# Two norm weights loaded as rows and spread by TensorE, in the input stage of a hybrid decoder block

## The chip, the cores and the metric

The kernel runs on one core of a Trainium2 chip. A core has TensorE (PE, with PEld for its weight loads), VectorE (DVE), ScalarE (ACT), GpSimd (POOL) and SyncE (SP, which here issues nearly all the loads), each with an instruction queue of its own that is worked off in order, and 16 DMA engines that they share. The metric is the device time of one execution in microseconds; the median over several executions counts. The profile is of one execution, and its span runs from the first instruction to the last.

## The reference

One decoder block on 1024 tokens of 1024 channels, all in float32: a state-space branch and a forgetting-attention branch read one normalised input, are gated and merged; then cross-attention into 256 memory tokens, a SwiGLU layer, and a last norm. What the change touches is the beginning:

```
def rms_norm(x, gain):
    y = xf * lax.rsqrt(jnp.mean(xf * xf, axis=-1, keepdims=True) + RMS_EPS)
    return (y * gain)
...
u = rms_norm(h, norm_mix[l])
proj = u @ w_in[l]
...
memory_cross_attention(..., rms_norm(mem, norm_mem_kv[l]), ...)   # k, v = split(m @ w_kv)
```

So the input stage normalises 256 memory tokens with the weight vector norm_mem_kv and 1024 tokens with norm_mix, both of 1024 channels, forms the keys and values of the memory, and the part of the input projection that the state-space branch reads.

## The kernel before

Products of full precision are made of three products of parts: each operand is split into a high part, rounded to TensorE's reduced float32 (a cast on ScalarE, L182), and a low part, the rest (a subtraction on VectorE, L183). `mm3` (L170 to L174) adds high x high, low x high and high x low.

The input stage (`stage_in`, from L344) works on ten tiles of 128 tokens by 1024 channels: memory tiles m and n, and tiles 0 to 7. A tile is loaded (F), its squares are summed on ScalarE (Q, L372), the root is taken on VectorE and GpSimd (R, L192 to L212), the tile is scaled by the root and the norm's weight on VectorE (S, L225; tiles 6 and 7 on ScalarE and GpSimd), turned on TensorE by eight products with the identity (T, L231, in two halves 0 and 1), and taken out of PSUM in high and low parts (E). Weight blocks are loaded (D) and split (W): blocks 0 to 3 for the keys (K, then k takes them out), 4 to 7 for the values (V, v), 8 to 11 for the state-space input (U, u). G loads a norm's weight vector, 0 for norm_mem_kv and 1 for norm_mix; y stores keys and values; L and P belong to the parameters of the state-space branch (L1192 to L1222, which turns them on TensorE at L1214 and L1221); X runs idle products with the identity (L250).

The order in which these steps are written is the string `ORDER_IN`. A scheduler then places the instructions on each engine's queue; a step that is written `behind` others is placed after them there. PSUM has banks of four kinds: three mm, two sc, two pv, one misc. All loads of the stage stand in SP's queue, and a load also waits for the one eight places ahead of it, and where its buffer is reused for the last reader of that buffer: of the weight buffers (raw) there are four, so block 4 waits for the split of block 0, block 5 for that of block 1.

A norm's weight is loaded by one DMA that reads the 4 KB vector for each of the 128 partitions, 512 KB into a tile:

```
S.dma_start(gain[i], (g_kv if i == 0 else g_mix).partition_broadcast(P))
```

## Time and profile before

| | |
|---|---|
| median of 3 runs | 1548.62 us (1547.12 to 1548.8) |
| the profiled execution | 1548.85 us |
| its span | 1547.1 us, 20406 instructions |
| TensorE busy | 1523.0 us, 98% |
| VectorE busy | 1010.4 us, 65% |
| ScalarE busy | 657.2 us, 42% |
| GpSimd busy | 255.1 us, 16% |
| moved by DMA | 235.10 MB, 152 GB/s in the mean |
| granted TensorE clock, mean | 0.997 |

A row of the windows gives a stretch of the span, its length, then the busy us and the number of instructions of PE, PEld, DVE, ACT and POOL, the granted clock, the busy share of the DMA engines (over 1 where transfers overlap) and GB/s. A row of waits gives who waited for whom, the us in total, the times and the longest. A row of the chain or of the timeline gives start and length in us, the engine, the line and what it does; in brackets the idle time ahead of it and what ended it. Lines in rows of before are those of the kernel before; in the changed kernel the same lines stand by one more up to the steps of the stage, and by some 30 more behind them.

### The profile page before, as it was taken

How to read it: one execution, taken by the hardware profiler on the slowest of the kernel's cores; microseconds unless marked ns; L12 is line 12 of the kernel's file. 1: busy time of each engine (PE TensorE's matmuls, PEld its weight loads, DVE VectorE, ACT ScalarE, POOL GpSimd, SP SyncE). 2: the span in 40 equal slices, each digit the busy share in tenths (PEclk: the TensorE clock that was granted, in tenths of full speed). 3: DMA queues.
4: the chain of work that ended last, by engine and by line, in shares of the span. 5: the costliest groups of instructions: out<-in, count | busy, mean ns of one | idle time of the engine just before them, and what ended most of it. 6: DMA issues, size and time to landing. Idle time of an engine off the chain costs nothing.

```text
span 1547.1 us, 20406 instructions
## 1 busy us (share of the span) xinstructions
PE 1523.0 (98%) x7325; PEld 1258.1 (81%) x7325; DVE 1010.4 (65%) x1824; ACT 657.2 (42%) x1178; POOL 255.1 (16%) x341
## 2 busy tenths in 40 slices
PE   8999999999999999999999999999999999999997
PEld 7788888898777678888888888888888888888886
DVE  6936554454778867675546797777777776665555
ACT  6424334323667643232425663333333333353342
POOL 1156442100211213200002200000000000100001
PEclk9999999999999999999999999999999999999999
DMA  9635557611224655369310256555554444896642
GB/s 310 160 103 103 130 121 140 190 35 17 47 47 90 172 149 185 109 202 314 110 69 1 109 205 204 160 160 161 162 160 158 156 144 146 296 391 208 195 151 108
DMA packets 196549, 235.10 MB, mean 152 GB/s; under 512 B 35592, under 2 KB 127656, under 8 KB 195936
## 3 DMA queue, kind: packets, MB, share of 16 engines
q1 hardware_dynamic: 188960, 215.97, 46.8%
q10 hardware_dynamic: 7488, 17.83, 3.1%
q8 instruction: 57, 0.93, 0.2%
q14 instruction: 44, 0.36, 0.1%
HBM read 162.98 MB, written 72.71 MB: 152 GB/s over the span
## 4 chain that ended last, share of the span: by engine, by line
PE 89%; DVE 5%; ACT 1%; issue 1%; DMA 1%; SPq 1%; POOL 0%; POOLq 0%; DVEq 0%; ACTq 0%
PE mm L898 15%; PE mm L172 9%; PE mm L174 9%; PE mm L173 9%; PE pv L898 8%; PE mm L1040 5%; PE sc L172 4%; PE sc L173 4%; PE sc L174 4%; PE sc L898 4%; PE sc L1040 4%; PE pv L1040 3%; PE misc L1040 2%; PE pv L172 1%; PE sc L1686 1%
## 5 line engine op out<-in xcount | busy, mean ns | idle before, releaser
L183 DVE TENSOR_TENSOR wlo<-raw,whi 128x1024 fp32r<-128x1024 f32 (+2 forms) x120 | 127.3, 1065 | 50.7 <-ACT whi L182 49.5
L182 ACT CAST whi<-raw 128x1024 fp32r<-128x1024 f32 (+2 forms) x120 | 108.5, 908 | 109.9 <-PE mm L173 41.2
L183 DVE TENSOR_TENSOR ol<-or,oh 128x1024 fp32r<-128x1024 f32 x73 | 89.9, 1234 | 73.0 <-ACT oh L182 72.3
L172 PE MATMUL mm<-uh,whi 128*128 128x512 f32 x344 | 137.2, 399 | 0.1
L173 PE MATMUL mm<-ul,whi 128*128 128x512 f32 x344 | 135.5, 394 | 0.0
L174 PE MATMUL mm<-uh,wlo 128*128 128x512 f32 x344 | 135.3, 394 | 0.0
L182 ACT CAST oh<-or 128x1024 fp32r<-128x1024 f32 x73 | 76.7, 1053 | 105.2 <-PE pv L1040 36.0
L931 POOL TENSOR_TENSOR g<-a,c 128x512 f32<-128x512 f32 x22 | 35.7, 1622 | 388.1 <-ACT a L930 388.1
L1696 POOL TENSOR_TENSOR pl<-pf,ph 128x512 fp32r<-128x512 f32 (+1 forms) x32 | 37.8, 1182 | 236.5 <-DVE ph L1695 197.3
L174 PEld LDWEIGHTS mm<-uh,wlo 128*128 128x128 f32 x344 | 65.0, 189 | 13.7 <-DVE wlo L183 0.5
L172 PEld LDWEIGHTS mm<-uh,whi 128*128 128x128 f32 x344 | 65.2, 189 | 12.0 <-DVE mc L1661 0.4
L173 PEld LDWEIGHTS mm<-ul,whi 128*128 128x128 f32 x344 | 65.2, 189 | 11.0
L202 POOL TENSOR_TENSOR r<-ms,mhalf 128x1 f32<-128x1 f32 (+1 forms) x30 | 20.4, 681 | 324.4 <-DVE ms L198 280.6
L920 DVE SCALAR_TENSOR_TENSOR c<-c,pv 128x512 f32<-128x512 f32 x22 | 15.1, 688 | 78.4 <-ACT c L919 78.4
L1693 ACT ACTIVATE pf<-sc 128x512 f32<-128x512 f32 (+1 forms) x96 | 46.4, 489 | 43.9 <-DVE sc L1689 27.8
L898 PE MATMUL pv<-S3h,we 128*128 128x512 f32 x176 | 57.8, 390 | 0.0
L1699 DVE TENSOR_TENSOR pl<-pf,ph 128x512 fp32r<-128x512 f32 (+2 forms) x64 | 35.3, 553 | 9.7 <-ACT ph L1698 9.1
L1040 PE MATMUL mm<-oh 128*128 128x512 f32 x106 | 41.3, 390 | 0.0
L1040 PE MATMUL mm<-ol,oh 128*128 128x512 f32 x106 | 41.3, 390 | 0.0
L1040 PE MATMUL mm<-oh,ol 128*128 128x512 f32 x106 | 41.3, 390 | 0.0
L172 PE MATMUL sc<-uh,whi 128*128 128x512 f32 x104 | 40.9, 393 | 0.0
L172 PE MATMUL mm<-yh,whi 128*128 128x512 f32 x104 | 40.8, 392 | 0.0
(595 smaller groups left out, 4559.3 us busy)
## 6 DMA issues: line engine op xcount, KB each, us to landing
or<-c_d SPq DMA_DIRECT2D x77, 256.0 KB
wo<-in_w_ffn_out_dram SPq DMA_DIRECT2D x22, 512.0 KB
c_d<-g SPq DMA_DIRECT2D x44, 256.0 KB
t_d<-wo SPq DMA_DIRECT2D x44, 256.0 KB
or<-t_d SPq DMA_DIRECT2D x44, 256.0 KB
rawb<-in_w_ffn_in_dram SPq DMA_DIRECT2D x20, 512.0 KB
raw<-in_w_ffn_in_dram SPq DMA_DIRECT2D x20, 512.0 KB
raw<-in_w_in_dram SPq DMA_DIRECT2D x19, 512.0 KB
```

What stands on the lines that cost most here:

```text
L172: T.matmul(ps, lh, rh, start=first, stop=False)
L173: T.matmul(ps, lh, rl, start=False, stop=False)
L174: T.matmul(ps, ll, rh, start=False, stop=last)
L182: cast = self.A.copy(hi, src)
L183: self.rest = (self.G if pool_lo else self.V).tensor_sub(lo, src, f32(hi))
L202: self.G.tensor_tensor(out=r, in0=v, in1=self.mhalf[:, 0:n], op=ALU.pow)
L898: T.matmul(ps, l_[:, k, :], r_, start=first and k == 0 and i == 0, stop=k == 3 and i == 2, skip_group_check=True)
L931: G.tensor_mul(g[:, 512:], a1, c1)
L1040: T.matmul(ps, l_[:, gi], r_[:, 512:], start=n < 3 and p == 0 and k == 0 or n == 7 and p == 0 and k == 0, stop=p == NP - 1 and k == 2, ski ...
L1693: self.exp = A.activation(pf[:, off:], ps[:, off:], AF.Exp)
L1696: G.tensor_sub(pl[:, off:], pf[:, off:], f32(ph[:, off:]))
L1699: V.tensor_sub(pl[:, off:], pf[:, off:], f32(ph[:, off:]))
```

## The change

Both weight vectors are loaded as one row of 4 KB into partition 0 of their tile (G). A new step B spreads a row over the partitions: TensorE multiplies a column of ones (a row of 128 ones as the stationary operand, plain float32) with the row, in two products of 512 columns, into two PSUM banks: mm for norm_mem_kv, sc for norm_mix. The memory tiles are scaled straight from PSUM, in two halves of 512 columns each. For norm_mix a new step C copies the two banks into the tile on ScalarE, behind the cast of the weight block last split (block 1). The squares of memory tile m are summed in two halves, one on ScalarE and one on VectorE. The 36 idle products become 10, and the turns of tile n use a bank mm in place of sc. In the order, memory tile n and block 0 are loaded ahead of norm_mix, B0 stands behind the idle products and B1 behind the turns of m, C1 ahead of token square 0, and E of m's first half ahead of the second turn of n.

```
 ORDER_IN = """
-Fm G0 Qm Fn D0 X36 Qn Rm D1 Sm F1 G1 Tm0 Tm1 Em0 Rn Sn Tn0 F0 D2 W0 Tn1 Em1 En0 En1 D3 F2 F3 W1 Q0 Q1 K0 D4 F4 F5 K1 R0
+Fm G0 Fn D0 G1 X10 B0 Qm Qn Rm D1 Sm F1 Tm0 Tm1 B1 Rn Sn Tn0 F0 D2 Em0 Tn1 W0 En0 Em1 En1 D3 F2 F3 W1 C1 Q0 Q1 K0 D4 F4 F5 K1 R0
 S0 T00 T01 k0 E00 Q2 W2 D5 F6 F7 E01 S1 T10 Q3 W3 k1 K3 K2 W4 E10 W5 D6 R1 k2 T11 k3 S2 Q4 V0 S3 T30
...
+    one = small.tile([1, P], F32, tag="one", bufs=1, name="one")
+    V.memset(one, 1.0)
     def gains(i):
         gain[i] = xtile("gain")
-        S.dma_start(gain[i], (g_kv if i == 0 else g_mix).partition_broadcast(P))
+        S.dma_start(gain[i][0:1, :], (g_kv if i == 0 else g_mix).rearrange("(o c) -> o c", o=1))
+
+    def spread_gain(i):
+        spread[i] = []
+        with B.behind(B.turning):
+            for b in range(2):
+                ps[i, "g", b] = B.bank(("mm", "sc")[i])
+                B.turning = T.matmul(ps[i, "g", b], one, gain[i][0:1, 512 * b:512 * b + 512], start=True, stop=True)
+                spread[i].append(ps[i, "g", b])
+
+    def keep_gain(i):
+        with B.behind(cast_w):
+            for b in range(2):
+                A.copy(gain[i][:, 512 * b:512 * b + 512], spread[i][b])

     def square(t):
...
+        if t == -2:
+            first = small.tile([P, 2], F32, name="ssm")
+            A.activation(junk[:, 0:512], tiles[t][:, 0:512], AF.Square, scale=1.0 / 32, accum_out=first[:, 0:1])
+            V.tensor_tensor_reduce(out=B.junk, in0=tiles[t][:, 512:], in1=tiles[t][:, 512:], scale=1.0 / D, scalar=0.0,
+                                   op0=ALU.mult, op1=ALU.add, accum_out=first[:, 1:2])
+            ss[t] = first
+            return
...
     def scale(t, pool):
         i = t // 2
         r = rs[t][:, 0:1] if t < 0 else rs[i][:, t % 2:t % 2 + 1]
-        with B.behind(turned_m if t == -1 else None):
-            scaled[t] = B.norm_scale(tiles[t], tiles[t], r, gain[0 if t < 0 else 1], pool=pool)
+        if t < 0:
+            for b in range(2):
+                h = tiles[t][:, 512 * b:512 * b + 512]
+                scaled[t] = B.norm_scale(h, h, r, spread[0][b])
+        else:
+            scaled[t] = B.norm_scale(tiles[t], tiles[t], r, gain[1], pool=pool)
```

The idle products and B are also placed one behind the other (`B.turning`). The order in which the instructions then stand differs on TensorE, VectorE, ScalarE and SP, all within the input stage. Four places:

SP's queue at the very start, before: memory tiles (xt from in_mem), the two weight vectors (gain), weight blocks (raw) and token tiles.

```order
L362 DMA xt<-in_mem_dram 128x1024
L366 DMA gain<-in_norm_mem_kv_dram 128x1024
L362 DMA xt<-in_mem_dram 128x1024
L403 DMA raw<-in_w_mem_kv_dram 128x8x128 x2
L362 DMA xt<-in_x_dram 128x1024
L366 DMA gain<-in_norm_mix_dram 128x1024
L362 DMA xt<-in_x_dram 128x1024
L403 DMA raw<-in_w_mem_kv_dram 128x8x128 x2
```

The same place of the changed kernel:

```order
L364 DMA xt<-in_mem_dram 128x1024
L372 DMA gain<-in_norm_mem_kv_dram 1x1024
L364 DMA xt<-in_mem_dram 128x1024
L433 DMA raw<-in_w_mem_kv_dram 128x8x128
L372 DMA gain<-in_norm_mix_dram 1x1024
L433 DMA raw<-in_w_mem_kv_dram 128x8x128
L364 DMA xt<-in_x_dram 128x1024 x2
L433 DMA raw<-in_w_mem_kv_dram 128x8x128 x2
```

Two loads of 128 rows became two of one row, and that of norm_mix went from behind the first token load to behind weight block 0; the order of the big loads is the same.

TensorE from the last idle product to the first key product (mh and ml are the turned memory tiles, whi and wlo a weight block), before:

```order
L250 MATMUL sc<-ident 128x256
L231 MATMUL misc<-ident,xt 128x128 x4
L231 MATMUL pv<-ident,xt 128x128 x4
L231 MATMUL sc<-ident,xt 128x128 x4
L231 MATMUL pv<-ident,xt 128x128 x4
L172 MATMUL mm<-mh_0_110,whi 128x256
```

and in the changed kernel:

```order
L252 MATMUL sc<-ident 128x256
L379 MATMUL mm<-gain,one 128x512 x2
L232 MATMUL misc<-ident,xt 128x128 x4
L232 MATMUL pv<-ident,xt 128x128 x4
L379 MATMUL sc<-gain,one 128x512 x2
L232 MATMUL mm<-ident,xt 128x128 x4
L232 MATMUL pv<-ident,xt 128x128 x4
L173 MATMUL mm<-mh_0_110,whi 128x256
```

B0 stands ahead of the turns of m, B1 between the turns of m and those of n.

ScalarE around weight blocks 4 and 5 (numbers of buffers kept, since the rows would read alike: before, raw_260 is block 4, raw_326 block 5, xt_262 and xt_264 are token tiles 4 and 5, uh are high parts of turned token tiles), before:

```order
L182 CAST uh0_0_87<-misc_300 128x2x128
L182 CAST kv_310<-mm_266 128x256
L182 CAST whi_399<-raw_260 128x1024
L372 ACTIVATE junk_109,ss2_431<-xt_262 128x1024
L182 CAST uh1_0_89<-misc_300 128x2x128
L182 CAST whi_407<-raw_326 128x1024
L182 CAST uh2_0_91<-pv_305 128x2x128
L372 ACTIVATE junk_109,ss2_431<-xt_264 128x1024
```

and in the changed kernel, where raw_250 is block 4, raw_316 block 5, and xt_252 and xt_254 are token tiles 4 and 5:

```order
L183 CAST uh0_0_87<-misc_290 128x2x128
L183 CAST kv_300<-mm_256 128x256
L183 CAST whi_389<-raw_250 128x1024
L183 CAST whi_397<-raw_316 128x1024
L183 CAST uh1_0_89<-misc_290 128x2x128
L398 ACTIVATE junk_109,ss2_421<-xt_252 128x1024
L183 CAST uh2_0_91<-pv_295 128x2x128
L398 ACTIVATE junk_109,ss2_421<-xt_254 128x1024
```

The cast of block 5 moved ahead of an evacuation of token tile 0 and of the square of token tile 4.

VectorE behind the split of block 5 (ss2_320 and ss2_431 hold the sums of squares of tiles 2 and 3, and of 4 and 5; xt_224 and xt_226 are tiles 2 and 3), before:

```order
L183 TENSOR_TENSOR wlo_408<-raw_326,whi_407 128x1024
L183 TENSOR_TENSOR ul2_0_99<-pv_305,uh2_0_91 128x2x128
L209 TENSOR_TENSOR rt2_415<-r02_414 128x2
L183 TENSOR_TENSOR ul0_0_95<-misc_337,uh0_0_87 128x2x128
L210 SCALAR_TENSOR_TENSOR rt2_415<-rt2_415,ms2_413 128x2
L183 TENSOR_TENSOR kv_311<-mm_349,kv_310 128x256
L183 TENSOR_TENSOR ul3_0_101<-pv_305,uh3_0_93 128x2x128
L211 SCALAR_TENSOR_TENSOR r02_414<-rt2_415,r02_414 128x2
L200 TENSOR_SCALAR ms2_471<-ss2_431 128x2
L225 SCALAR_TENSOR_TENSOR xt_224<-xt_224,r02_414,gain_175 128x1024
```

and in the changed kernel, with the sums of tiles 2 and 3 in ss2_310 and of 4 and 5 in ss2_421, and tile 2 in xt_212:

```order
L184 TENSOR_TENSOR wlo_398<-raw_316,whi_397 128x1024
L184 TENSOR_TENSOR ul2_0_99<-pv_295,uh2_0_91 128x2x128
L201 TENSOR_SCALAR ms2_403<-ss2_310 128x2
L201 TENSOR_SCALAR ms2_461<-ss2_421 128x2
L184 TENSOR_TENSOR ul0_0_95<-misc_327,uh0_0_87 128x2x128
L210 TENSOR_TENSOR rt2_405<-r02_404 128x2
L184 TENSOR_TENSOR kv_301<-mm_339,kv_300 128x256
L184 TENSOR_TENSOR ul3_0_101<-pv_295,uh3_0_93 128x2x128
L211 SCALAR_TENSOR_TENSOR rt2_405<-rt2_405,ms2_403 128x2
L210 TENSOR_TENSOR rt2_463<-r02_462 128x2
L212 SCALAR_TENSOR_TENSOR r02_404<-rt2_405,r02_404 128x2
```

The first step of the root of tiles 4 and 5, which needs both their sums of squares, moved ahead of three splits and of the root of tiles 2 and 3.

17 lines of the change are left out of this document (11 added, 6 removed).

## The prediction

> **What bounds the kernel now.** I read the page's busy rows first, then the table of windows over the first 40 us, then TensorE's waits, and last the chain that ended last, in order of time.
>
> ```profile
> PE 1523.0 (98%) x7325; PEld 1258.1 (81%) x7325; DVE 1010.4 (65%) x1824; ACT 657.2 (42%) x1178; POOL 255.1 (16%) x341
> 10.00:20.00 10.00, 6.76 (x42) 6.32 (x43) 8.17 (x14) 6.93 (x12) 0.70 (x1) 0.83 1.08 370
> 20.00:30.00 10.00, 9.58 (x81) 9.21 (x80) 7.66 (x12) 8.29 (x16) 0.70 (x1) 1.00 1.04 402
> 30.00:40.00 10.00, 9.01 (x49) 7.07 (x47) 10.00 (x24) 7.41 (x18) 1.71 (x1) 1.00 0.95 187
> ```
>
> TensorE (PE) is busy for 98% of the span; what it idles lies for the most part in the first 62 us, in the stage that is changed. Behind that the two programs have the same instructions in the same order, so a shift of TensorE at 62 us should reach the end unchanged. In that stage the DMA engines are full from 10 to 30 us (shares 1.08 and 1.04), and VectorE (DVE) from 30 to 40 us (10.00 of 10). TensorE's waits behind the first products, and the chain:
>
> ```profile
> PE sc L231 <- DVE xt L225: 2.8, 1, 2.8
> PE misc L231 <- DVE xt L225: 1.0, 1, 1.0
> PE misc L1214 <- PE mm L173: 0.8, 1, 0.8
> ...
> 16.82 10.66 DMA raw<-in_w_mem_kv_dram
> 27.50 1.06 ACT whi L182
> 28.59 1.23 DVE wlo L183
> ...
> 33.38 1.20 DVE xt L225
> 34.72 0.63 PE misc L231 x4
> 52.52 0.77 issue
> 53.28 0.23 PE misc L1214
> ```
>
> The chain does not run through the start. It runs through the queue of loads: weight block 5 (step W5, the second block of values) lands at 27.5 us, ScalarE (ACT) casts it, VectorE works through splits and scalings without a pause, and TensorE, which had its own work done at 33.7, turns token tile 3 at 34.72. From there it is busy to 52.5 us. So the question is how much earlier that turn comes.
>
> **The loads: -2.8 us at W5.** Two loads of 512 KB (both norm weights spread over 128 partitions by the DMA) become two of 4 KB; both stood ahead of block 5. What the loads move per us:
>
> ```profile
> 4.00:8.00 4.00, 4.00 (x23) 2.94 (x22) 1.55 (x5) 1.17 (x3) 1.27 (x4) 1.00 1.00 323
> 24.00:27.50 3.50, 3.15 (x28) 2.97 (x27) 2.34 (x6) 1.79 (x4) 0.44 (x1) 1.00 1.04 416
> ```
>
> 1.05 MB at 416 GB/s is 2.5 us, at 323 GB/s 3.2 us; I take 2.8 (some 370 GB/s, as from 10 to 20 us). It holds only if the queue never runs dry. Block 5 is issued when VectorE has split block 1, which I put at about 16.1 us; four loads then still stand ahead of it, over 5 us of transfer. So block 5 lands at 24.7.
>
> **The start: about -0.9 us.** These rows carry it:
>
> ```profile
> 4.50 1.06 ACT L372 ACTIVATE junk<-xt 128x1024 bf16<-128x1024 f32 x1 [2.41 <-DMA xt<-in_mem_dram]
> 7.08 1.28 DVE L225 SCALAR_TENSOR_TENSOR xt<-xt,r,gain 128x1024 f32<-128x1024 f32 x1
> 7.98 1.06 ACT L372 ACTIVATE junk<-xt 128x1024 bf16<-128x1024 f32 x1 [2.33 <-DMA xt<-in_mem_dram]
> 9.14 0.58 ACT L182 CAST mh<-misc 128x512 fp32r<-128x512 f32 x1
> 12.39 0.66 PE L231 MATMUL sc<-ident,xt 128*128 128x128 f32 x4 [2.84 <-DVE xt L225]
> L1661 DVE CUSTOM_DVE_ANT_0 junk<-mm,tri 128x512 bf16<-128x512 f32 x16 | 10.9, 683 | 1.6 <-PE mm L1659 1.3
> ```
>
> The first memory tile m still lands at 4.4. Its sum of squares is now two halves side by side, about 0.58 on ScalarE (as the cast of 512) and 0.68 on VectorE (as the 512-wide reduction with an accumulator), so its root is ready at 6.65 instead of 7.08. The second tile n lands near 6.2 instead of 7.95, since 0.52 MB less is ahead of it at 323 GB/s. What may eat this are the four added products of a row of ones with the weight row, plain fp32 and 512 wide. No such product stands in the trace; the nearest rows are these:
>
> ```profile
> 147.23 0.39 PE L1471 MATMUL pv<-St,Gm 128*128 128x128 f32 x2
> 147.45 0.39 PE L1470 MATMUL pv<-xg,Tt 128*128 128x128 f32 x2
> ...
> 30.41 0.39 PE L174 MATMUL sc<-whi,ml 128*128 128x512 f32 x1
> 30.64 0.40 PE L172 MATMUL sc<-whi,mh 128*128 128x512 f32 x1
> ```
>
> A plain fp32 product is two records and 0.224 us per 128 columns, so at most 0.90 us for 512; two records at the 0.23 us of the 512-wide row give at least 0.46. I take 0.90, since L1470 and L1471 are the nearest plain fp32 rows. A start falls in a slow stretch of TensorE; the idle matmuls alone, in two windows, with the count as what tells the rate:
>
> ```profile
> 1.86:4.20 2.34, 2.34 (x12) 1.00 0.94 266
> 7.40:8.40 1.00, 1.00 (x11) 1.00 1.14 334
> ```
>
> That is 12 in 2.34 us at first and 11 in 1.00 at the end, half the rate, though the column of the granted clock says 1.00 for both. So I double the price in B0, to 1.8 us. Beside this row, the Trainium skill (FP8 and Floating Point Precision, section TensorE Precision Notes) has true fp32 as four passes through the array; by that it would be 4 x 0.23 = 0.92, and the sum stays as it is.
>
> B0 (two products) then runs from 4.6 to about 8.0. The first bank is ready in time; the second holds up the second half of m, scaled by 8.75 (before: 8.36). VectorE's next work follows: n's root, then n's halves, done at about 11.95 (12.25 before). TensorE turns n's first half at about 11.4, against 12.39. If the products cost the lower bound, it is about 10.3. B1, behind m's turn, fits before n is scaled.
>
> **ScalarE: +1.05, then 1.3 lost to the order.** C1 copies the spread row of norm_mix from PSUM, two copies of 512 at a spacing of about 0.5, ahead of token square 0; half a square (0.48) is gone. Before, this stretch of ScalarE had slack:
>
> ```profile
> 16.64 1.05 ACT L182 CAST whi<-raw 128x1024 fp32r<-128x1024 f32 x1 [0.49 <-DMA raw<-in_w_mem_kv_dram]
> 19.76 1.06 ACT L372 ACTIVATE junk<-xt 128x1024 bf16<-128x1024 f32 x1 [0.33 <-DMA xt<-in_x_dram]
> 20.82 1.03 ACT L182 CAST whi<-raw 128x1024 fp32r<-128x1024 f32 x1
> 25.04 1.06 ACT L372 ACTIVATE junk<-xt 128x1024 bf16<-128x1024 f32 x1 [0.66 <-DMA xt<-in_x_dram]
> 27.50 1.05 ACT L182 CAST whi<-raw 128x1024 fp32r<-128x1024 f32 x1 [1.05 <-DMA raw<-in_w_mem_kv_dram]
> 28.72 1.06 ACT L372 ACTIVATE junk<-xt 128x1024 bf16<-128x1024 f32 x1
> ```
>
> Followed by hand through the new order, ScalarE casts W3 at 19.45 (before 20.82), the copies being paid out of the 0.49 and 0.33 of waiting for loads, and reaches W5 at 23.3, so it still waits for the load until 24.7. But the cast of W5 now stands ahead of a token evacuation and square 4, which used to run while block 5 was under way. Behind the cast come 0.27 + 1.05 + 0.27 (spacings of the same rows) and then square 5, whose sum is read 3.7 us after the landing; VectorE has the root's first step of that sum ahead of tile 2's root and of three splits. From the landing to token tile 3 scaled I count 8.5 us; it was 34.72 - 27.50 = 7.2. So 1.3 of the 2.8 us is lost, and the turn comes at 33.2: **-1.5 us**. TensorE's own work, carried along, is done at about 32.9, so it still waits, and 1.8 is the most that this place gives.
>
> Behind it, VectorE and ScalarE have the same work as before, all earlier by 1.5. The wait of 0.8 at L1214 (52.5 to 53.3) ends with VectorE's last split out of the bank that it writes:
>
> ```profile
> 52.76 0.42 DVE L183 TENSOR_TENSOR ul<-misc,uh 128x256 fp32r<-128x256 f32 x1 [0.44 <-ACT uh L182]
> ```
>
> So it moves along with that engine: 0. The 26 idle matmuls dropped ran while the first loads were under way: 0, unless the clock (below) goes with them. So 1548.85 for the profiled execution becomes 1547.35; the median of the runs is 0.23 below that execution, which gives 1547.1, and I say **1547.2**.
>
> **Rivals.**
>
> *The loads pass through whole (chance 0.20).* These times go from the median, 1548.62. If W5's place costs nothing, because square 5's sum is not what VectorE waits for, the gain is 2.8: 1545.8; if the 0.8 at L1214 closes too, 3.6: 1545.0. For it: the chain above. Against it: VectorE's 10.00 of 10 and the new order.
>
> *ScalarE becomes the bound (0.12).* If block 5 lands only 0.7 us earlier (its issue follows the split of block 1, which I have only 0.3 to 0.7 earlier), the 1.3 of W5's place outweighs it, by 0.6, and the 1.05 of copies finds no slack left: +1.6, and 1548.62 + 1.6 = 1550.2. It decides where the landing moves by less than 1.3. Against it: DMA shares over 1 say that bytes bound the landings and not issues.
>
> *The clock (0.06).* The granted clock as the trace has it:
>
> ```profile
> 15.00:16.00 1.00, 1.00 (x6) 1.00 (x7) 1.00 (x2) 1.00 (x3) 0.00 (x0) 0.50 1.18 290
> 17.00:18.00 1.00, 1.00 (x8) 1.00 (x7) 0.29 (x1) 1.00 (x2) 0.00 (x0) 0.66 1.16 349
> ```
>
> Half clock costs the 256-wide products 0.21 us each instead of 0.12, 6 in a us against the 11 above; some 18 products paid it in 3.4 us. If with 10 idle matmuls all 48 of the first two keys pay it, that is 30 x 0.095 = 2.9 us more on TensorE, less 0.9 of start and 1.0 of the wait at 34.72: +1.0, 1549.6. It is the case that ends slower, and decides from where TensorE and not VectorE is last at tile 3, some 0.3 us beyond my forecast. The Trainium skill speaks against the change here (TensorE: Matmul & The Clock Gate, section What's actually happening): full clock comes after about 3.4 us of activity, in a window that runs by itself. The half clock that the rows above show before 17.7 is short enough to agree with that length. What speaks against the rival: the four wide products keep TensorE busy in place of the idle matmuls.
>
> **How the numbers follow.** My forecast has 0.62, with 1546.3 to 1548.3 for landings that move by 2.0 to 3.2 us. Up to 0.2%, 3.1 us, a measurement of this kernel can't well be told from no change. The whole-pass rival gives half its chance beyond that, and the forecast's far end 0.05: faster 0.15. The two slower rivals lie within 0.2% but for their far ends: slower 0.04; same 0.81. The range is 1545.3 to 1549.7: it holds the whole-pass case but for its last 0.8 (0.07 left out) and the clock's case; the ScalarE case lies beyond it (0.10 left out).
>
> **What would show it.** Right: the cast of W5 waits for its load and starts near 24.7; square 5 follows 2.5 us later; TensorE turns token tile 3 near 33.2 after waiting for its scaling; two records of B0 take 1.8 us each pair or less; everything past 62 us is earlier by one constant. Wrong: no idle time of ScalarE ahead of W5 (ScalarE bounds), a half clock past 18 us, a turn of tile 3 at or before 32, or a new wait of TensorE between 35 and 62 us.

## The result and the profile after

The changed kernel takes 1551.98 us in the median of 15 runs (1548.49 to 1555.63), the kernel before 1548.56 in 15 runs beside it. The ratio is 1.0021, with an interval of 1.0015 to 1.0028: slower by 0.2%, some 3.4 us. The profiled execution took 1553.78 us (span 1552.1), 4.9 more than that of before; it lies 1.8 above its own median, so the pieces below add up to more than 3.4.

The busy row of the page and the table of windows, changed kernel:

```profile
PE 1528.8 (99%) x7307; PEld 1257.5 (81%) x7307; DVE 1016.4 (65%) x1829; ACT 658.2 (42%) x1180; POOL 256.9 (17%) x341
10.00:20.00 10.00, 9.86 (x31) 6.46 (x30) 6.64 (x11) 6.09 (x11) 0.05 (x1) 1.00 1.09 363
20.00:30.00 10.00, 9.77 (x80) 9.35 (x79) 8.82 (x14) 9.56 (x18) 0.70 (x1) 1.00 0.90 327
```

TensorE is busy for 5.8 us more with 18 matmuls fewer. From 10 to 20 us it does 31 where it did 42 (the column of the clock reads 1.00 there, but the trace's first clock record comes at 20.46, and the 256-wide products ahead of it follow each other in 0.21 us, behind it in 0.12: half rate until then). ScalarE is busy for 9.56 us of the next ten where it was for 8.29. The DMA engines, full from 20 to 30 us before (1.04, 402 GB/s), are at 0.90 and 327 (0.57 and 209 from 26 to 28): the queue of loads runs dry there. TensorE's waits:

```profile
PE pv L1502 <- ACT Tt L1437: 1.7, 1, 1.7
...
PE mm L1691 <- DVE mc L1696: 1.2, 1, 1.2
...
PE misc L1246 <- PE mm L174: 0.7, 1, 0.7
...
PE misc L232 <- DVE xt L226: 0.2, 1, 0.2
```

The waits of 2.8 for memory tile n and of 1.0 for token tile 3 are gone. In their place stand two that the kernel before does not have, and both lie far behind the changed stage: 1.7 at L1502 (149.6 us) and 1.2 at L1691 (421.6 us). TensorE's timeline at the start shows where the first gain went:

```profile
4.82 3.75 PE L379 MATMUL mm<-gain,one 1*128 1x512 f32 x4 [0.64 <-DMA gain<-in_norm_mem_kv_dram]
8.50 1.11 PE L232 MATMUL misc<-ident,xt 128*128 128x128 f32 x4
10.45 3.78 PE L379 MATMUL sc<-gain,one 1*128 1x512 f32 x4
14.16 1.12 PE L232 MATMUL mm<-ident,xt 128*128 128x128 f32 x4
15.95 0.58 PE L173 MATMUL mm<-mh,whi 128*128 128x256 f32 x1
```

Both pairs of row products take 3.75 us or more. The second stands ahead of the turn of n, so that turn starts at 14.16 (before: 12.39), though n is scaled at 12.66. ScalarE, which takes the turned tile out of PSUM, waits for it; before, and then in the changed kernel, with the cast of weight blocks 4 and 5:

```profile
13.08 0.58 ACT L182 CAST mh<-sc 128x512 fp32r<-128x512 f32 x1 [1.92 <-PE sc L231]
```

```profile
15.31 0.59 ACT L183 CAST mh<-mm 128x512 fp32r<-128x512 f32 x1 [3.65 <-PE mm L232]
...
25.97 2.01 ACT L183 CAST whi<-raw 128x1024 fp32r<-128x1024 f32 x2
```

From 15.31 on ScalarE has pauses of 0.27 and 0.44 us only, until blocks 4 and 5 are cast one behind the other, with no waiting for a load. Block 5 lay ready by then: the last of the sixteen semaphore updates of its load comes at 24.73 in the trace, and its cast starts at 26.92. Before, they came at 27.48 and 27.50. So the load landed 2.75 us earlier, and its cast began only 0.6 earlier. On TensorE, token tile 3 is turned at 35.91 (before: 34.72), with no waiting either:

```profile
35.91 0.63 PE L232 MATMUL misc<-ident,xt 128*128 128x128 f32 x4
```

Following the same TensorE instruction in both traces gives a ladder of its lateness: +1.6 us at 53, +0.8 at 115, +2.6 at 147, +2.7 at 335, +4.2 at 517, +5.1 at 546, +4.9 at the end. So there are three pieces: some 0.8 from the input stage, some 1.8 between 115 and 147 us, 1.2 at 420 us, and a rest near 546. A ladder is of one execution: TensorE's granted clock falls near 360 us in some (0.83 from 355 to 365 us in that of before, 0.84 in that of the change) and not in others (1.00), which alone is worth some 1.3 us there: a kernel below that has no such fall goes from 0.1 ahead at 335 us to 1.5 ahead at 417. So the pieces are read from 53 to 335 us and from the waits.

### The profile page after: what moved, and what is told of

The parts are those of the page before. It is cut to its first block, busy times and chain, and to the rows that moved or that the text cites. A ratio compares the mean times of both kernels' runs of the same rounds, so it can differ in the third digit from the quotient of the medians.

```text
span 1552.1 us, 20382 instructions
## 1 busy us (share of the span) xinstructions
PE 1528.8 (99%) x7307; PEld 1257.5 (81%) x7307; DVE 1016.4 (65%) x1829; ACT 658.2 (42%) x1180; POOL 256.9 (17%) x341
## 4 chain that ended last, share of the span: by engine, by line
PE 86%; DVE 6%; DMA 3%; ACT 2%; issue 2%; POOL 1%; SPq 0%; POOLq 0%; DVEq 0%; ACTq 0%
PE mm L930 15%; PE mm L173 8%; PE mm L175 8%; PE mm L174 8%; PE pv L930 8%; PE mm L1072 5%; PE sc L930 4%; PE sc L1072 4%; PE sc L173 3%; PE sc L174 3%; PE sc L175 3%; PE pv L1072 3%; PE misc L1072 2%; DMA rb<-rd_d 1%; PE pv L173 1%
## 5 line engine op out<-in xcount | busy, mean ns | idle before, releaser
L1191 POOL TENSOR_TENSOR sg<-sg,ga 128x512 f32<-128x512 f32 x16 | 29.6, 1874 | 73.0 <-DVE sg L1184 73.0
```

The costliest lines, as they stand in the source:

```text
L1191: self.B.G.tensor_mul(self.out[j][:, cs], self.out[j][:, cs], ga)
```

## The experiments

Two theories stood at first. By the one, the input stage makes the loss: the row products bring no clock, so the keys run at half rate up to 20.5 us. By the other, the stage is nearly neutral and the shift lands badly behind it. The first kernels tell these apart. In all of the kernels below the whole computation is done; idle products and extra loads write to places that nobody reads.

**The loads spread by the DMA again, without row products** (the halves and the 10 idle products stay):

```diff
-Fm G0 Fn D0 G1 X10 B0 Qm ... Tm0 Tm1 B1 Rn ... W1 C1 Q0
+Fm G0 Fn D0 G1 X10 Qm ... Tm0 Tm1 Rn ... W1 Q0
-        S.dma_start(gain[i][0:1, :], (g_kv if i == 0 else g_mix).rearrange("(o c) -> o c", o=1))
+        S.dma_start(gain[i], (g_kv if i == 0 else g_mix).partition_broadcast(P))
-                scaled[t] = B.norm_scale(h, h, r, spread[0][b])
+                scaled[t] = B.norm_scale(h, h, r, gain[0][:, 512 * b:512 * b + 512])
```

> The changed kernel, but both norm weights come again as 512 KB loads spread over 128 partitions; the four products with ones (steps B0, B1) and the two copies (C1) are gone. The halves, the new order and the 10 idle matmuls stay. Theory A (the four one-row products cost the time: they hold TensorE at half clock and push the first key product from 13.72 to 15.95 us): first key product back at 13.0 to 14.2 us, token tile 3 turned at 34.7 to 36, time 1548.0 to 1550.0, ratio to before 0.9997 to 1.0009. Theory B (the loss is made behind 60 us by whatever shifts the start, so any kernel with this order loses it): ratio stays at 1.0015 or more though the first key product is early. Theory C (the 26 idle matmuls dropped are the cause): half clock past 18 us here too, first key product near 14 us but 48 key products at half rate, ratio about 1.001 to 1.002.

Measured: 1548.22 beside 1548.57, ratio 1.0000 (0.9991 to 1.0009). On the ladder it is 1.7 us ahead of before at 115 us and 0.1 ahead at 546: without the row products the loss is gone, but a gain of the stage does not reach the end either.

**The kernel before with 10 idle products:**

```diff
-Fm G0 Qm Fn D0 X36 Qn Rm
+Fm G0 Qm Fn D0 X10 Qn Rm
```

> The kernel before with 10 idle matmuls instead of 36, nothing else. Theory C (idle matmuls are the cause): turn of m at half rate (1.1 us for four instead of 0.6), key products at half rate for 3 to 5 us longer, turn of token tile 3 at 35.5 or later, ratio 1.0007 to 1.002. Theory A (only the one-row products matter): the half clock lasts past 18 us perhaps, but TensorE waits for VectorE at tile 3 anyway, so the turn stays at 34.7 to 35.2 and the ratio at 0.9995 to 1.0006. Theory B: like A at 62 us, and a ratio that goes by what happens behind it.

Measured: 1549.12, ratio 1.0004 (0.9995 to 1.0013). On the ladder: 1.6 ahead at 115 us, 0.7 behind at 546. The number of idle products changes more than their own time: the scheduler places the turns of the tokens otherwise. What the stage wins is again lost far behind it.

**The kernel before, its idle products one row high** (36 as before, in the same order on each engine):

```diff
-        one = self.ident.bitcast(BF16)
+        one = self.ident.bitcast(BF16)[0:1, :]
```

> The kernel before with its 36 idle matmuls taken over one partition (1x128 by 1x256) instead of 128; nothing else. They last as long and keep TensorE as busy. If the height of the product is what the clock goes by (theory A's reason for the half clock of B0 and B1): 4 to 5 idle matmuls per 0.5 us to the end of the stretch, which then ends near 9.8 us instead of 8.5 and delays the turn of m, which takes 1.1 us for four turns; half clock on the key products past 18 us. If height is nothing to the clock: as before, 7 per 0.5 us from 7.5 us on, stretch over at 8.5, turns at 0.60 for four, ratio 1.0000 within 0.0005.

Measured: 1548.16, ratio 1.0000 (0.9991 to 1.0009). TensorE's timeline of this kernel:

```profile
1.87 7.86 PE L250 MATMUL sc<-ident 1*128 1x256 bf16 x36 [1.87 <-POOL ident masks.py:199]
9.65 1.11 PE L231 MATMUL misc<-ident,xt 128*128 128x128 f32 x4
15.16 0.58 PE L172 MATMUL mm<-mh,whi 128*128 128x256 f32 x1
```

Products of one row keep TensorE busy for 7.9 us and it stays at half rate (36 in that time, 0.22 us each): the turn of m behind them takes 1.11 us, as behind the row products of the changed kernel. (The Trainium skill, page TensorE: Matmul & The Clock Gate, section What's actually happening, says that the hardware doesn't count instructions and that about 3.4 us of activity bring the full clock. Here 7.9 us of it, one row high, did not; the measurement decides.) The first key product comes 1.4 us later than before, and the time is the same. A late start and a half clock up to 19.5 us cost nothing in the kernel before, where ScalarE still waits 0.48 us for block 5 and casts it at 27.30.

**The changed kernel with 24 idle products ahead of B0:**

```diff
-Fm G0 Fn D0 G1 X10 B0 Qm
+Fm G0 Fn D0 G1 X24 B0 Qm
```

> The changed kernel with 24 idle matmuls instead of 10; nothing else. At half rate 24 end near 7.4 us, so the products of B0 start there instead of at 4.8. Theory A in the form that the clock was never raised because full activity ended at 4.2 us: the four records of B0 take 1.9 us (0.93 a product) instead of 3.75, those of B1 1.9, m's turn comes near 9.5 us, the first key product near 14.0 instead of 15.95, at full clock or nearly; ratio 0.999 to 1.001. Theory A in the form that one-row products pull the clock down by themselves: B0 begins quick, B1 is back at 3.75 us, first key product at 15 to 16.5, ratio 1.001 to 1.003. Theory B: the ratio stays near 1.002 either way.

Measured: 1548.90, ratio 1.0002 (0.9993 to 1.0011). B0 now takes 1.98 us, at full clock, but behind it the clock falls: it is 0.5 from 9.73 us on, while m is still being turned. So B1 takes 3.78 us again, and the first key product starts at 15.99, as in the changed kernel. Yet the loss is nearly gone: the ladder shows 0.0 at 115 and 147 us, and only the wait of 1.2 at L1691 is still there. The clock in the first 20 us is not what costs 3.4 us.

**The changed kernel and the kernel before again, in another batch:**

> The changed kernel once more, on the chip of the first four experiments, for a second profile and a second comparison. So far the start does not explain the time: the kernel before with one-row idle matmuls started its key products 1.4 us late at half clock and took 1548.2, and the changed kernel with 24 idle matmuls started them as late as the changed kernel (15.99 us) and took 1548.9. Theory B1 (what lies behind 60 us was chance of that execution and that chip): median 1548.5 to 1550, and no wait of TensorE for Tt near 148 us. Theory B2 (the order that the scheduler chose with 10 idle matmuls, met by a start 2.2 us late, costs the 3 us each time): median 1551 to 1553, first L1419 turn at 116.1 again (0.8 behind before), and part of the loss made again between 115 and 150 us and between 400 and 550 us.

> The kernel before, once more, for a second profile: which of its times behind 60 us are the same each time. If the pieces behind 60 us are chance, then the store of the last u block, the drop of the granted clock near 355 us and the waits of TensorE between 500 and 550 us differ from the first profile by 1 us or more in all; if not, all marks are within 0.3 us of the first profile's.

Measured: the changed kernel 1552.01 beside 1548.21, ratio 1.0028 (1.0017 to 1.0039), with 2.3 at L1502 and 1.2 at L1691; one execution of the kernel before took 1548.54, and up to 370 us its TensorE marks stand within 0.3 us of those of the first profile. So the two new waits belong to the kernel and not to one execution. The first can cost more than its length: in this second profile the granted clock is 0.5 for 3.4 us from 150.8, right behind the wait, and the lateness is 3.3 at 147 and 5.1 at 335.

**The row products over all 128 rows** (zeros but for row 0 in both operands):

```diff
-    one = small.tile([1, P], F32, tag="one", bufs=1, name="one")
-    V.memset(one, 1.0)
+    one = small.tile([P, P], F32, tag="one", bufs=1, name="one")
+    V.memset(one, 0.0)
+    V.memset(one[0:1, :], 1.0)
...
+        V.memset(gain[i], 0.0)
-                B.turning = T.matmul(ps[i, "g", b], one, gain[i][0:1, 512 * b:512 * b + 512], start=True, stop=True)
+                B.turning = T.matmul(ps[i, "g", b], one, gain[i][:, 512 * b:512 * b + 512], start=True, stop=True)
```

> The changed kernel, but the products that spread the weight rows are of full height: the row of ones is the first of 128 rows of which the others are zero, and so is the weight row (VectorE fills both with zeros in its idle time ahead of 4 us). Count, form and order of the instructions on TensorE, ScalarE, GpSimd and SP are the same as in the changed kernel; VectorE has three fills more at the start. If the height of the product is what the clock goes by: B0 slow at first, clock up near 7.5 us as before the change, B1 in 1.9 us instead of 3.78, first key product at 13.8 to 14.4 us instead of 15.95, half clock over before 18 us. The time then tells what the late start costs in this order: theory A (the start costs it): 1548.5 to 1549.5, ratio 0.9995 to 1.0008. Theory B (it is lost behind 60 us whatever the start): 1551 to 1552.5, ratio above 1.0014. If height is nothing to the clock: start as in the changed kernel.

Measured: 1552.06, ratio 1.0021 (1.0012 to 1.0030). The timelines of TensorE and ScalarE in this kernel:

```profile
10.36 1.98 PE L381 MATMUL sc<-gain,one 128*128 128x512 f32 x4 [0.33 <-DMA gain<-in_norm_mix_dram]
13.67 0.39 PE L173 MATMUL mm<-mh,whi 128*128 128x256 f32 x1
35.68 0.63 PE L232 MATMUL misc<-ident,xt 128*128 128x128 f32 x4 [0.28 <-DVE xt L226]
```

```profile
26.96 1.04 ACT L183 CAST whi<-raw 128x1024 fp32r<-128x1024 f32 x1 [2.30 <-DMA raw<-in_w_mem_kv_dram]
```

With 128 rows the clock rises, B1 takes 1.98, and the first key product starts at 13.67, as in the kernel before; the time is that of the changed kernel. So an early start by itself does not bring the 3.5 us back. It is not a clean test of the input stage, though, since the fills hold up the first loads: SP waits 1.1 us for a fill ahead of the first weight row and issues weight block 1 at 4.49 (changed kernel: 2.98), and from 4 to 8 us the loads move 227 GB/s (there: 292). So block 5 lands late here, at 26.89, its cast waits for it, and token tile 3 is turned at 35.68, 0.96 later than before, behind VectorE. No kernel has both the early start and the early loads.

**The kernel before with only the halves** (square of m on two engines, memory tiles scaled in two halves from the tile that the DMA spread):

```diff
+        if t == -2:
+            first = small.tile([P, 2], F32, name="ssm")
+            A.activation(junk[:, 0:512], tiles[t][:, 0:512], AF.Square, scale=1.0 / 32, accum_out=first[:, 0:1])
...
+        if t < 0:
+            for b in range(2):
+                h = tiles[t][:, 512 * b:512 * b + 512]
+                scaled[t] = B.norm_scale(h, h, r, gain[0][:, 512 * b:512 * b + 512])
```

> The kernel before with the memory tiles squared (the first one) and scaled in halves, and nothing else: both weights by 512 KB loads, 36 idle matmuls. Theory A and the rivals of the prediction alike have this part as a small gain at the start: m's turn at 8.0 to 8.6 us (idle matmuls run to 8.5), n's first half turned some 0.6 us earlier, 11.6 to 12.0 us, first key product 12.9 to 13.3 instead of 13.72, and block 5 at 27.5 as before, so that the turn of token tile 3 stays at 34.5 to 34.9: ratio 0.9995 to 1.0005. Theory B (order chosen by the scheduler): the ratio may be off by up to 0.002 either way without a difference at the start.

Measured: 1549.63, ratio 1.0010 (1.0001 to 1.0019). Token tile 3 is turned at 36.13 (before: 34.72), the ladder shows +1.4 at 53 and at 115 us, and it keeps that to 546 (+1.3). Here a loss in the input stage, with the other order that the scheduler gives, passes through to the end.

### The piece at 147 us: where the instruction fetch falls

The state-space input is stored (u_d) and read back in another layout (xg). SP issues the first xg load when the last u_d store has landed. In most kernels that is 2.7 us behind the issue of the store, in the changed one 4.6. The table of half us, changed kernel:

```profile
97.50:98.00 0.50, 0.50 (x4) 1.00 0.76 311
98.00:98.50 0.50, 0.50 (x4) 1.00 0.06 8
...
99.50:100.00 0.50, 0.50 (x4) 1.00 0.04 16
```

The kernel before:

```profile
97.50:98.00 0.50, 0.50 (x4) 1.00 0.00 0
```

Before, nothing moves any more at 97.5. Now 0.06 of the 16 engines, that is one of them, goes on alone for two us. What went ahead of it is in the list of DMA queues for the window from 94 to 101 us of the changed kernel, and not in that of 93 to 99 of the kernel before:

```profile
q8 instruction: 1, 0.02, 1.5%
```

This is a piece of TensorE's instructions. The trace has 57 such packets of 16 KB for 14614 records of matmuls and weight loads, one for some 256, and in all 17 profiles the fourth of them starts when 898 to 913 of these records have begun, be that at 89 us or at 98. It takes one DMA engine away from the store: from 96.60 to 98.30, while it runs, the store has at most 15 packets under way at a time (before: 16), and behind it the store's last eight packets follow one by one, up to 99.91.

In the kernel before the piece is fetched at 92 us, between the two u_d stores; the changed kernel has 18 matmul and 18 weight-load records less ahead of it, so its stream reaches the next piece later, at 96 us, within the store. From there SP's queue, ScalarE and VectorE tell the rest. SP before, and then in the changed kernel:

```profile
97.73 5.25 SPq L1412 DMA_DIRECT2D xg<-u_d  x8
124.15 5.05 SPq L1400 DMA_DIRECT2D Ts<-Ts  x3
133.20 0.98 SPq L157 DMA_DIRECT2D raw<-in_w_in_dram  x2
```

```profile
100.43 3.55 SPq L1444 DMA_DIRECT2D xg<-u_d  x7
129.17 4.67 SPq L1432 DMA_DIRECT2D Ts<-Ts  x3
137.84 0.99 SPq L158 DMA_DIRECT2D raw<-in_w_in_dram  x2
```

A shift of 2.7 at the first xg load has become 5.0 at Ts and 4.6 at the gate's weights (raw). VectorE shows what made it grow, first before, then in the changed kernel:

```profile
117.76 0.42 DVE L1373 TENSOR_TENSOR d<-ES,trg_cs 128x256 f32<-128x256 f32 x1
...
123.81 0.28 DVE L1397 TENSOR_TENSOR Ts<-misc,dbc 128x128 f32<-128x128 f32 x1
```

```profile
121.75 1.10 DVE L1407 TENSOR_TENSOR EC<-d,d 128x256 f32<-128x256 f32 x1
122.88 1.26 DVE L1405 TENSOR_TENSOR d<-ES,trg_cs 128x256 f32<-128x256 f32 x1
...
128.83 0.28 DVE L1429 TENSOR_TENSOR Ts<-misc,dbc 128x128 f32<-128x128 f32 x1
```

Of the six 256-wide steps, four took 0.42 us before; now five take 1.1 to 1.3. GpSimd waits for TensorE in this place and so is late by only 0.8, VectorE's steps by 2.7, and now they meet: from 118.8 to 126.6 us the two take turns, one instruction each. ScalarE then copies Tt, which TensorE needs, behind a cast that waits for raw. Before, and then in the changed kernel:

```profile
141.33 1.05 ACT L182 CAST whi<-raw 128x1024 fp32r<-128x1024 f32 x1 [1.37 <-DMA raw<-in_w_in_dram]
...
142.77 1.04 ACT L1405 COPY Tt<-Ts 128x1024 f32<-128x1024 f32 x1
```

```profile
147.06 1.05 ACT L183 CAST whi<-raw 128x1024 fp32r<-128x1024 f32 x1 [5.24 <-DMA raw<-in_w_in_dram]
...
148.50 1.03 ACT L1437 COPY Tt<-Ts 128x1024 f32<-128x1024 f32 x1
```

The copy is 5.7 us late. Before, it ended at 143.8 and TensorE came at 147.0, a slack of 3.2; TensorE itself is late by 0.8; 5.7 - 3.2 - 0.8 is the wait of 1.7.

Three kernels move the fetch, each in another way.

**The changed kernel with more and smaller row products** (each in four of 128 columns, and two more idle products: the stream of TensorE is longer, the work nearly the same):

```diff
-Fm G0 Fn D0 G1 X10 B0 Qm
+Fm G0 Fn D0 G1 X12 B0 Qm
-                B.turning = T.matmul(ps[i, "g", b], one, gain[i][0:1, 512 * b:512 * b + 512], start=True, stop=True)
+                for c in range(0, 512, 128):
+                    e = min(c + 128, 512)
+                    B.turning = T.matmul(ps[i, "g", b][:, c:e], one, gain[i][0:1, 512 * b + c:512 * b + e], start=True, stop=True)
```

> The changed kernel with each of its four row products cut into four of 128 columns (same columns in all, so the same time on TensorE), and 12 idle matmuls instead of 10, which fit into the gap of 0.64 us ahead of B0 and keep the scheduler's order: otherwise all engines have the changed kernel's instructions in its order. TensorE's stream is 52 instructions longer, as long as before the change. Theory F (the place of the 16 KB instruction fetches is what costs): the fetch near 96 us comes near 92 us again, the u store lands 2.4 us after its issue, no wait for Tt near 148 us, the wait for the exponentials near 545 us falls from 0.6 to 1.7 us to about 0.3, with the start as late as in the changed kernel (first key product near 16 us); what stays is 0.8 from the input stage and 1.2 near 420 us: 1549.0 to 1550.2. Theory A or B2 (start and order): 1551.3 to 1552.7. Theory R: no change, as the loads are the same.

Measured: 1549.33, ratio 1.0007 (0.9998 to 1.0016). The fetch is at 89 us (the stream is 52 records longer than the changed kernel's and 16 longer than that of before), and the copy of Tt comes 0.9 us earlier than before:

```profile
141.87 1.04 ACT L1439 COPY Tt<-Ts 128x1024 f32<-128x1024 f32 x1
```

The wait at L1502 is gone; that at L1691 (1.2) is not. The ladder: -0.4 at 115 and at 147, +0.5 at 546. Since the start gained 1.2 too against the changed kernel (B0 ran partly at full clock), not all of the 2.7 us between the two is the fetch.

**The kernel before with a shorter stream and nothing else** (17 idle products of 512 columns in place of 36 of 256):

```diff
-Fm G0 Qm Fn D0 X36 Qn Rm
+Fm G0 Qm Fn D0 X17 Qn Rm
-            self.T.matmul(ps[:, :2 * P], one[:, :P], one, start=True, stop=True)
+            self.T.matmul(ps.rearrange("p (a b) -> p a b", a=2), one[:, :P], one.unsqueeze(1).to_broadcast([P, 2, 2 * P]),
+                          start=True, stop=True)
```

> The kernel before with its 36 idle matmuls of 256 columns taken as 17 of 512 (5% fewer columns, over at some 8.2 us instead of 8.5, ahead of the first scaling's end at 8.36); all else the same, in the same order. TensorE's stream is 38 instructions shorter. Theory F: the fetch of 92 us comes near 95.9, into the last u store (95.4 to 97.3): landing 3.5 us or more after the issue instead of 2.35, the fetch of 530 us comes near 535 and the wait for the exponentials near 541 us grows from 0.24 to 0.6 to 1.6: 1549.3 to 1551.5, ratio 1.0005 to 1.002, with the start and the input stage as before. All other theories: 1548.5, ratio 1.0000 within 0.0006.

Measured: 1549.24, ratio 1.0010 (1.0001 to 1.0019). With no row load and no row product in it, the fetch falls at 96 us, the xg load comes 4.6 us behind the store, and the new wait is there:

```profile
147.44 0.49 PE L1471 MATMUL pv<-xg,Tt 128*128 128x128 f32 x2 [1.43 <-ACT Tt L1406]
```

Its input stage had gained 1.2 us at 115; at 147 it is 0.4 late. This is the plainest of the runs: 19 idle products fewer, and a gain of 1.2 becomes a loss, 90 us after the last of them.

**Sixteen rows instead of one in the weight load** was meant for the other late wait (below), on the theory that a load in a single piece delays one DMA engine's queue:

```diff
-        S.dma_start(gain[i][0:1, :], (g_kv if i == 0 else g_mix).rearrange("(o c) -> o c", o=1))
+        S.dma_start(gain[i][0:16, :], (g_kv if i == 0 else g_mix).partition_broadcast(16))
```

> The changed kernel with each weight row loaded into 16 partitions instead of 1 (16 times the same 4 KB; only the first is used). All engines have the same instructions in the same order. A one-row load is a single piece, and all other loads near it are cut into 16 or a multiple. Theory R (the odd piece shifts which of the 16 DMA engines gets which part of every later transfer; that is why the spread 1/sum lands late near 419 us in every kernel with row loads, and why one part of the last u store trails): no wait of 1.2 us for the row maximum near 420 us, the u store lands within 2.5 us of its issue, and the time is 1548.5 to 1550. Theory F (TensorE has 52 instructions fewer, so its instruction fetches of 16 KB come some 4 us later and one of them meets the last u store): unchanged, 1551.3 to 1552.7, with the store again 3.5 to 4.3 us under way.

Measured: 1553.01, ratio 1.0033 (1.0020 to 1.0045). A miss: the wait of 1.2 at L1691 stays. The load in 16 pieces lands later, which makes the start 0.8 to 1.1 us later than in the changed kernel and moves the store, but the fetch is within it again: 2.0 at L1502. (The changed kernel's stream is 36 records shorter than that of before, by the page, and not 52.)

**Both edits:**

> The last two edits of the changed kernel together: rows loaded into 16 partitions, and row products cut into four with 12 idle matmuls. Theory R and F each for its part: neither the late u store nor the wait near 420 us nor the long one near 545 us; what is left is the input stage, 0.5 to 0.8 us behind before at 115 us: 1548.6 to 1549.5, ratio 1.0000 to 1.0007. If R is wrong and F right: as with the cut products alone, 1.2 us more. If both are wrong: 1551.3 to 1552.7.

Measured: 1551.12, ratio 1.0018 (1.0010 to 1.0027). The fetch is out of the way (91 us) and no wait stands at L1502; the late start of the 16 rows costs 1.9 on the ladder at 115 and 147, and L1691's 1.2 comes on top.

Four kernels keep the changed kernel's order on every engine up to 115 us and move its start. Against the changed kernel:

| kernel | first key product | lateness at 115 |
|---|---|---|
| split | -1.14 | -1.2 |
| split, one load (below) | +0.07 | +0.1 |
| 16-row load | +0.89 | +0.9 |
| 16-row load, split | +1.15 | +1.1 |

In this order the stage hands a shift of its start on whole. The loads have landed by the time ScalarE comes to them, and no wait for a load is left to take the shift up, as there was in the kernel before with one-row idle products.

### The piece at 420 us: a hiccup of SP's queue

In the attention, SP stores the reciprocals of a head's denominators (rd_d) and loads them back spread over 64 partitions (rb); VectorE multiplies with them. SP before, and then in the changed kernel:

```profile
410.25 0.35 SPq L1731 DMA_DIRECT2D rd_d<-rc  x1
411.74 0.51 SPq L1733 DMA_DIRECT2D rb<-rd_d  x1
412.64 0.40 SPq L1606 DMA_DIRECT2D raw<-in_w_in_dram  x1
```

```profile
413.06 0.36 SPq L1763 DMA_DIRECT2D rd_d<-rc  x1
414.90 0.50 SPq L1765 DMA_DIRECT2D rb<-rd_d  x1
415.46 0.57 SPq L1638 DMA_DIRECT2D raw<-in_w_in_dram  x1
```

From store to load it is 1.49 before and 1.84 after; from the load to the next issue 0.90 and 0.56. A pause of 0.35 us has moved from behind the rb load to ahead of it. VectorE and GpSimd, before:

```profile
415.57 1.21 DVE L1739 TENSOR_TENSOR num<-num,rb 64x1024 f32<-64x1024 f32 x1
415.73 2.20 POOL L1696 TENSOR_TENSOR pl<-pf,ph 128x512 fp32r<-128x512 f32 x1 [2.80 <-DVE ph L1695]
```

And in the changed kernel, with TensorE:

```profile
418.53 1.29 POOL L1728 TENSOR_TENSOR pl<-pf,ph 128x512 fp32r<-128x512 f32 x1 [2.80 <-DVE ph L1727]
418.99 1.91 DVE L1771 TENSOR_TENSOR num<-num,rb 64x1024 f32<-64x1024 f32 x1 [0.54 <-DMA rb<-rd_d]
421.56 0.44 PE L1691 MATMUL mm<-hb 68*128 68x384 f32 x1 [1.24 <-DVE mc L1696]
```

Whichever of the two starts first has its plain time (1.21 or 1.29), the second stands still until the first is done: 2.20 for GpSimd before, 1.91 for VectorE now. (The Trainium skill, SBUF — State Buffer, section Terms, says that the pair of memory ports which VectorE and GpSimd share is held for a whole instruction and that the loser blocks; these rows agree.) GpSimd's delay cost nothing. VectorE's makes the reduction behind it (mc) late, and TensorE waits 1.24. So 0.35 us on an idle queue became 1.24 on TensorE by who came first.

The wait stands in seven of the eight profiles of kernels that load the weights as rows and spread them with products (the eighth follows), and in none of the others. Their SP queue has one wait more than before: the tile that a later weight block reuses was last read by TensorE. Counted from the start, the pause lies between the 207th and the 208th instruction of SP's queue in the kernel before as in the changed one; with one instruction more ahead of it, another instruction of this place is the one held up. Two kernels try that with a load of 8 bytes more on SP.

**One load more in the split kernel:**

```diff
+        if n == 1:
+            S.dma_start(small.tile([1, 2], F32, tag="extra", bufs=1, name="extra"), g_mix[0:2].rearrange("(o c) -> o c", o=1))
```

> The changed kernel with cut row products and 12 idle matmuls (as in the run that took 1549.33), and one load of 8 bytes more on SP near 60 us, into a tile that nobody reads. All other instructions and their order are the same. Theory S (SP's stream has a hiccup of 0.34 us at a fixed place, between the wait for the stored 1/sum and the load that spreads it, because the changed kernel has one wait more on SP than the kernel before; the load comes 0.34 us late, VectorE's scaling starts after GpSimd's subtraction instead of ahead of it, takes 2.3 us instead of 1.2, and TensorE waits 1.24 us near 418 us): with one instruction more the hiccup falls into the time in which SP waits for the store anyway, the load is issued 1.49 us or less after the store instead of 1.85, the wait of 1.24 is gone, time 1547.8 to 1548.6. Rival (the row products themselves, or the banks they take, cause that wait): it stays, 1549.0 to 1549.8.

Measured: 1548.67, ratio 1.0005 (0.9996 to 1.0013). SP's queue:

```profile
411.32 0.35 SPq L1767 DMA_DIRECT2D rd_d<-rc  x1
412.74 0.50 SPq L1769 DMA_DIRECT2D rb<-rd_d  x1
```

It is 1.42 from store to load, and the wait at L1691 is gone with row loads and products all present. The time is 0.7 below that of the split kernel, taken in another batch, less than the two tell apart, and the profiled execution has a wait of 1.2 near 547 us that the split kernel has not. The trace shows the mechanism; its worth in time was not resolved.

**One load more in the kernel before:**

> The kernel before with one load of 8 bytes more on SP near 60 us, into a tile that nobody reads; nothing else. Theory S: the hiccup of SP falls between the wait for the stored 1/sum and the load that spreads it (1.84 us from store to load instead of 1.49), and the wait of TensorE of 1.24 us for the row maximum near 417 us appears, with everything ahead of 400 us as before: 1549.4 to 1549.9, ratio 1.0005 to 1.0009. Rival: no such wait, 1548.5, ratio 1.0000.

Measured: 1548.47, ratio 1.0000 (0.9992 to 1.0009). A miss: the expected wait did not come. From store to load it is 1.43, not 1.84. The extra load also turned the round of DMA semaphores by one, so that the wait for the store no longer is an instruction of its own ahead of the load. That the pause sits at a count of instructions, and that this place decides the wait, is supported by the seven profiles and by the kernel with the extra load; the forecast made from it failed in this one.

The pause is not the only one of its kind. Behind records 79, 207, 335 and so on of SP's queue, one in 128, each of the 17 profiles has a gap of 0.34 us or more (0.05 is usual from one record to the next), and a packet of 8 KB of the kind "instruction" starts 0.05 to 4.1 us behind each of them. Since 16 KB are some 256 of TensorE's records, 8 KB would be 128. So the pause is probably the change from one piece of SP's own instructions to the next; no run tests it.

### A version meant to keep the gain

**The first experiment (weights spread by the DMA, halves, 10 idle products) with 24 idle products one column wide**, which only lengthen TensorE's stream:

```diff
+            for _ in range(24):
+                self.turning = self.T.matmul(ps[:, :1], one[:, :P], one[:, :1], start=True, stop=True)
```

> A version that may beat both: halves and the changed kernel's order, but both weights by 512 KB loads (the first experiment, 1548.22), with 24 idle matmuls of a single column behind the 10, so that TensorE's stream is 48 instructions longer; order kept but for three turns of 128 columns that move past one product each. Theory F (the place of the 16 KB fetches): the first experiment was 1.7 us ahead of before at 115 us and lost 1.5 of it near 541 us, where a fetch at 536.5 us fell on the transfers of the row maxima; here that fetch comes near 532, the loss is gone, and the time is 1546.5 to 1547.3, ratio 0.9988 to 0.9993. Without theory F: 1548.2.

Measured: 1547.20 beside 1548.62, ratio 0.9993 (0.9984 to 1.0002). The fetches move to 91 and 530 us, and the 1.6 us gained at 115 are still there at 546 (1.5). It is the lowest median of all, but the interval does not exclude no gain.

All kernels side by side. Lateness is on TensorE against the profile of before; "fetch" is the microsecond in which TensorE's piece of instructions comes near the store; "store to xg" runs from the issue of the last u_d store to that of the first xg load; the waits are TensorE's (at L1502, at L1691 for mc, and the longest for pf).

| kernel | median, ratio | at 115 | fetch | store, to xg | L1502 | L1691 | pf | at 546 |
|---|---|---|---|---|---|---|---|---|
| before | 1548.56 | 0 | 92 | 95.1, 2.7 | none | none | 0.5 | 0 |
| changed | 1551.98, 1.0021 | +0.8 | 96 | 95.8, 4.6 | 1.7 | 1.2 | 0.6 | +5.1 |
| changed, again | 1552.01, 1.0028 | +0.8 | 96 | 95.9, 4.3 | 2.3 | 1.2 | 1.7 | +6.9 |
| 128 rows | 1552.06, 1.0021 | +0.5 | 96 | 95.6, 3.9 | none | 1.2 | 1.6 | +5.0 |
| 16-row load | 1553.01, 1.0033 | +1.6 | 98 | 96.7, 4.6 | 2.0 | 1.2 | 1.4 | +6.8 |
| 16-row load, split | 1551.12, 1.0018 | +1.9 | 91 | 96.9, 2.7 | none | 1.2 | 0.5 | +3.4 |
| split | 1549.33, 1.0007 | -0.4 | 89 | 94.7, 2.7 | none | 1.2 | 0.5 | +0.5 |
| split, one load | 1548.67, 1.0005 | +0.9 | 91 | 96.0, 2.7 | none | none | 1.2 | +2.2 |
| 24 idle | 1548.90, 1.0002 | 0.0 | 92 | 95.1, 2.7 | none | 1.2 | 0.5 | +1.0 |
| before, 17 wide idle | 1549.24, 1.0010 | -1.2 | 96 | 93.9, 4.6 | 1.4 | none | 0.5 | +0.7 |
| before, halves | 1549.63, 1.0010 | +1.4 | 93 | 96.4, 2.7 | none | none | 0.5 | +1.3 |
| before, one-row idle | 1548.16, 1.0000 | -0.2 | 91 | 94.9, 2.7 | none | none | 0.5 | -2.0 |
| before, 10 idle | 1549.12, 1.0004 | -1.6 | 96 | 93.5, 2.7 | none | none | 1.2 | +0.7 |
| DMA spread | 1548.22, 1.0000 | -1.7 | 96 | 93.4, 2.7 | none | none | 1.3 | -0.1 |
| DMA spread, padded | 1547.20, 0.9993 | -1.6 | 91 | 93.5, 2.7 | none | none | 0.5 | -1.5 |
| before, one load | 1548.47, 1.0000 | -0.1 | 92 | 95.0, 2.6 | none | none | 0.5 | +0.2 |

The column "store, to xg" has two values: 3.9 to 4.6 in the five profiles whose fetch comes 0.5 to 2.5 us behind the issue of the store, and 2.6 or 2.7 in the eleven whose fetch comes earlier, or (twice, 93.4 and 93.5) at 96 us when the store has landed. With 128 rows the wait at L1502 is missing although the store was late: its copy of Tt ended at 147.40, just as TensorE came.

Near 546 us the wait for pf is 1.2 or longer in six profiles. In five of them a later fetch falls between 536 and 542 us; but the kernel with 17 wide idle products has a fetch at 536 and no such wait, the first profile of the changed kernel has one at 540 and a wait of 0.6, and the split kernel with one load has the wait with its fetch at 530. No run tests this place by itself. Its cause is open.

## Why the prediction was wrong

Forecast 1547.2, measured 1551.98. The step that failed is in the first part: "Behind that the two programs have the same instructions in the same order, so a shift of TensorE at 62 us should reach the end unchanged." The order is the same, and TensorE's lateness still changed from 0.8 at 115 us to 4.9 at the end. What differs is the length of the streams: TensorE's is shorter by 18 pairs of records, so that a fetch falls into a store; SP's is longer by a wait, so that a pause falls ahead of a load. Against the forecast of -1.5, the input stage is off by 2.3 (+0.8 at 115), what lies behind it by 4.1 in the profiled execution.

The terms of the sum, in their order:

- **The loads: -2.8 us at W5.** The landing was right: 24.73 for 24.7, 2.75 earlier than before, though the load was issued at 18.98 and not at 16.1, behind VectorE's late split of block 1. What was wrong is that ScalarE would be waiting for it.
- **The start: about -0.9 us.** B0 was right: 3.75 for 3.6, with the turn of m at 8.50. B1 is the term of the stage that failed. It was priced at 1.8, full clock (it is 1.98 where the clock is full), and called free behind the turn of m. It took 3.78, since products of one row do not bring the clock, and the turn of n came at 14.16 and not at 11.4. ScalarE, waiting for that turn, casts block 1 at 16.65 (before: 14.04) and does not catch up. A start 1.4 us late cost nothing in the kernel before, but in the changed kernel's order a shift of the start passes on whole. What B1 alone is worth was not measured.
- **ScalarE: +1.05, then 1.3 lost to the order.** ScalarE casts block 3 at 22.90 and not at 19.45, and never waits for block 5: it comes to it at 26.92. That is the sign set down for the ScalarE rival ("no idle time of ScalarE ahead of W5"). From there to the turn of token tile 3 it is 9.0 us, 8.5 foreseen, so that the turn comes at 35.91 and not at 33.2.
- **The wait of 0.8 at L1214 moves along: 0.** About right: 0.7, 1.6 us later.
- **26 idle matmuls dropped: 0, unless the clock goes.** Wrong in a way that neither branch held: by themselves they moved the order of the tokens' turns (the kernel before with 10 of them is 1.6 ahead at 115) and the place of the fetch (the one with 17 wide ones).

Of the rivals, the whole pass (1545.8) had the landing right and fails all the same, since it was ScalarE and not the load that was last at W5. The clock did fall short, up to 20.5 us, as its rival had it; half clock alone was worth nothing in the kernel before, and in the changed kernel no run separates it from the place of B1. The ScalarE rival (1550.2, +1.6) has the right sign at W5 but not its condition, a landing that moves by less than 1.3; it has the right size at 53 us (+1.6), but of that only 0.8 remain at 115. No rival had the two waits at 149.6 and 421.6 us, which together bring 2.9 of the 4.9 us in the profiled execution. The chance of slower, 0.04, was therefore much too small.

## What to carry to other kernels

A stretch that keeps its instructions and their order does not keep its time: adding or dropping instructions far ahead of it moves the points where TensorE's instructions are fetched and where SP pauses, and each can land on a transfer that others wait for. Look for the fetch (queue "instruction" of the DMA view) near each store or load on the critical path before and after, and try a few idle products more or less before judging a change of some us; here 24 of one column moved a median from 1548.22 to 1547.20, though the two intervals overlap. And before counting an earlier landing as time, see when the engine that takes the load is free: here block 5 landed 2.75 us earlier and was cast 0.6 us earlier.
